# A decoder block on one core: VectorE's weight low parts booked beside GpSimd in the planner, and the last query tile's scores as three products of 352 columns

## The chip, the cores and the metric

One core of one Trainium2 chip. The metric is the device time of one execution in microseconds; the time before is 654.11 us, the median of three runs (653.83 to 655.35).

## What is computed

One transformer block on 512 tokens of width 1024, all in float32: a norm, projections, two kinds of attention, output projection with norm and residual, a gated feed-forward part with a short convolution (width 2816), and an embedding gate (PLE). What matters here is the attention with compressed, selected and window branches ("nsa", 8 heads in 2 groups), and the sliding-window attention ("swa", 8 heads in 2 groups):

```python
s_c = einsum(q, k_cmp) * scale - slope * dist_c      # 31 compressed keys
p_c = softmax(s_c) * valid_c                         # o_c = p_c @ v_cmp
s_s = einsum(q, k_selected) * scale - slope * dist   # causal; 512 tokens have 8 blocks, all are selected
s_w = einsum(q, k_window) * scale - slope * dist     # causal, window 512
o = g0 * o_c + g1 * o_s + g2 * o_w
...
mix = concat(o_nsa, o_swa) @ w_o
x = x + rmsnorm(mix); h = rmsnorm(x); gu = h @ w_gate_up
```

## The kernel before

**Arithmetic.** A float32 operand is split into a high part, rounded to the matmul's own format, and a low part, the rest; a product is three matmuls, high x high, low x high, high x low. ScalarE makes a weight's high part (`hi`, `oh`), VectorE or GpSimd subtracts it from the raw weight to give the low part (`lo` at L1056 for 1024 columns; `low` at L967 for 512 columns of the output projection, on GpSimd for its first half and on VectorE for its second).

**Units.** Attention runs as 16 units, `ORDER`: the nsa kind before the swa kind, group 0 before group 1, and query tiles of 128 tokens in the order 3, 0, 2, 1. A unit has four heads r. For each head TensorE makes scores (`s`, L584 and L585: the query against the keys' high and low parts), VectorE adds the distance bias and takes the minimum in one pass (`m`, `soft`, L588: a custom operation and a read of its accumulator), ScalarE exponentiates in place (`e`, L592), VectorE takes reciprocals (`rc`, L689, L755), and GpSimd scales the rows (`g`, `scale_rows`, L580). Then, block by block of 128 keys, TensorE transposes four heads' probabilities (`t`, L782), ScalarE makes the high part (`h`, L786), VectorE the low part (`l`, L790), and TensorE multiplies by the values (`v`, L797). The unit's sum is added up, split (`up`, `ad`, `oh`, `ol`; L840, L847, L852, L856) and kept for the output projection. GpSimd also normalizes the compressed branch (`px`, `gc`, `pm`).

In an nsa unit the key tiles `kn` lie as 32 compressed keys, then 512 keys of one branch, then 512 of the other, 1056 columns in a row. For query tile 3 (units 0 and 4) the scores of one head are three products into three PSUM banks: 256 columns, of which the first 32 are used, and twice 512. VectorE takes three passes: over 32, 512 and 512 columns.

**Fill work.** Beside the units TensorE has matmuls of large rank that it runs when nothing of the units is ready: projections of queries and keys (`f`, L247 to L251; ended by `fe`, then moved to other partitions by 4 or 8 transfers `fm` on SP, L924), the output projection's first half, which needs the nsa mixes alone, and its second half with the swa mixes (`op`, L976 to L978; phases "fill" and "outproj"), and the eight PLE products of six matmuls (`pl`, L1087 to L1090). Loads go over SP's queue (`w` L883, `ow` L959, `ld` L1049, `x1` L1073). After the units come the squares and their sum (`sq`, `sa`), the norm's column and row (`col` L1110, `row` L1123), per chunk `n1`, `n2`, `nh` (L1140), `nl`, `nq`, and the first gate and up products (`ma`, L1163).

**The planner.** From the start of the units to those products, the order of the work is made by a list scheduler in the kernel's own code (`Plan`, with `add` and `order`). Each operation has an engine, an estimated length, a rank, what it comes after, and the buffers that it takes and uses. A step picks, on each engine, the operation of lowest rank that can start when the engine is free (otherwise the one that can start first), and emits over all engines the one that starts first. The estimates decide the order alone: every engine runs its queue in that order, and waits on the chip only for data and buffers. The ranks of the units count in units: about i - 1 + r/4 for scores and softmax of unit i, i and more for its products; fill has 1000 and more. `SHIFT` adds to a rank below 100, by the first letters and the length of an operation's name: ("hi", 2) is the high part of the norm's weights, ("e", 4) an nsa exponential, ("e", 3) an swa one, ("pe2", 2) the eviction of a PLE product. The high parts of the norm's weights have ranks 15.0, 15.2 and 15.4 for p and the two PLE weights and 16.5 to 17.1 for the first gate and up weights before the shift; `lo` is 0.1 behind.

Of the kernel before, what the change touches and what calls it, by code (L numbers as in the profile page):

```python
# [15 lines left out]
P = 128  # L16
# [46 lines left out]
PAIRS = 2  # L63
UNITS = 3
SHIFT = {("px", 2): 0.26, ("sa", 2): -0.78, ("l", 4): 0.71, ("pe2", 2): -1.35, ("v", 4): 1.33, ("e", 4): 1.34,
         ("ol", 3): -0.84, ("oe", 3): 0.38, ("ol", 2): 1.32, ("e", 3): 0.21, ("sq", 2): -0.62, ("s", 4): 0.18,
         ("pm", 2): 1.23, ("t", 3): 0.43, ("lo", 2): -0.03, ("oh", 3): -0.25, ("hi", 2): 0.71}
# [7 lines left out]
class Plan:  # L75

# [14 lines left out]
    def add(self, name, eng, us, rank, f, after=(), take=(), use=(), land=0.0):  # L91
# [3 lines left out]
        self.ops[name] = (eng, us, rank, f, [a for a in after if a], list(take), land)  # L95
# [5 lines left out]
    def order(self, free):  # L101
# [28 lines left out]
        while len(out) < len(ops):  # L130
            best = None
            for eng, names in todo.items():
                pick, f = None, free.get(eng, 0.0)
                for name in names:
# [3 lines left out]
                    t = max(r, f)  # L138
# [10 lines left out]
            free[eng] = t + op[1]  # L149
            done[name] = t + op[1] + op[6]  # L150
# [21 lines left out]
class Block:  # L172
# [136 lines left out]
    def move(self, dst, src):  # L309
        self.nc.sync.dma_start(dst.bitcast(F32), src.bitcast(F32))  # L310
# [283 lines left out]
    def plan_units(self, plan, qready):  # L594
# [10 lines left out]
        for i, (kind, g, qt) in enumerate(units):  # L605
# [32 lines left out]
            if kind == "n":  # L638
# [5 lines left out]
                segs = {0: [(0, 160, 2)], 3: [(0, 256, 1), (NCMP, T, 1), (NCMP + T, T, 1)]}.get(  # L644
                    qt, [(0, NCMP + n, 1), (NCMP + T, n, 1)])
                for r in range(4):
# [18 lines left out]
                    for b, seg in enumerate(segs):  # L665
# [7 lines left out]
                    where = {0: [(0, 0, NCMP), (0, NCMP, n), (0, 160, n)], 3: [(0, 0, NCMP), (1, 0, n), (2, 0, n)]}.get(  # L673
                        qt, [(0, 0, NCMP), (0, NCMP, n), (1, 0, n)])
                    for b, (sb, c0, w) in enumerate(where):

                        def soft(r=r, b=b, sb=sb, c0=c0, w=w, u=u, per=per, n=n, slope=slopes[r], bias=(cb if b == 0 else bias)):
                            dst = u["pc"][:, r, :] if b == 0 else u["pk", r // per][:, r % per, b - 1, :n]
                            self.soft(dst, u["ps", r, sb][:, c0 : c0 + w], bias, slope, 3e38, u["nm"][:, r, b : b + 1])

                        op(("m", i, r, b), "DVE", soft_us(w), x + 0.01 * (b == 2), soft, [("s", i, r, sb)], (), [("ps", i, r, sb)])
# [190 lines left out]
    def plan_projections(self, plan, order, due, given):  # L872
# [4 lines left out]
        for n, f in enumerate(order):  # L877
# [65 lines left out]
            for m in range(moves):  # L943
                a(("fm", f, m), "SP", 0.5, rank - 50, lambda m=m, move=move: move(m), [("fe", f, 2)],
                  [("u", ("q", f))] if m == 0 and f != 8 else [], [("ft", f)], land=1.8)
# [776 lines left out]
```

## Time and profile before

| | us |
|---|---|
| median of three runs | 654.11 |
| the profiled execution | 655.55 |
| its span, from the first to the last instruction | 653.8 |
| TensorE busy | 641.0 (98%) |
| VectorE busy | 483.6 (74%) |
| ScalarE busy | 365.2 (56%) |
| GpSimd busy | 148.7 (23%) |
| mean granted clock of TensorE | 0.995 of full speed |

PE is TensorE, DVE VectorE, ACT ScalarE, POOL GpSimd, SP the engine that only issues transfers. The units run from about 74 to 220 us; the first gate and up products begin at 249.6 us. A matmul's length in the rows is longer than its pitch, since matmuls overlap: pitches are read from start to start. Each row of a timeline is: start in us, length in us (of all instructions that it merges, xN), engine, line, operation, tiles written and read, shapes, and in brackets the idle time before it and what ended it.

### The profile page before, as it was taken

The page shows a single profiled execution, that of the slowest core. Times are in us where ns is not written, and L with a number is a line of the kernel's source. Part 1 is how long each engine was busy: PE and PEld are TensorE (multiplying, and loading weights), DVE is VectorE, ACT ScalarE, POOL GpSimd, SP SyncE. Part 2 cuts the span into 40 slices and gives each one's busy share as a digit, 9 for nine tenths or more (in the row PEclk, how much of TensorE's full clock was granted, in tenths as well). Part 3 has the DMA queues.
Part 4 walks back from the last instruction along what each step waited for, and adds up shares of the span by engine and source line. Part 5 has one row for each costly group of instructions (what it writes and reads, how often), then busy time and mean ns, then how long its engine had stood idle before and what let it go on. Part 6 is the DMA issues. An engine that isn't in the chain of part 4 may idle for free.

```text
span 653.8 us, 10319 instructions
## 1 busy us (share of the span) xinstructions
PE 641.0 (98%) x3709; PEld 562.3 (86%) x3709; DVE 483.6 (74%) x994; ACT 365.2 (56%) x709; POOL 148.7 (23%) x223
## 2 busy tenths in 40 slices
PE   8999999999998999999998999999999999999996
PEld 7988888888886888888888999999998888889985
DVE  6794769988896469689899999999857333233972
ACT  6554779889998366265555556556636322222341
POOL 1112597668476230021320000000000000010000
PEclk9999999999999999999999999999999999999999
DMA  8437623110236159203323334233263454331031
GB/s 300 149 118 222 180 81 85 45 50 26 72 106 234 48 178 321 97 34 96 130 97 119 91 115 129 71 125 129 57 201 113 145 217 126 110 96 65 1 131 63
DMA packets 27282, 78.01 MB, mean 119 GB/s; under 512 B 3424, under 2 KB 4704, under 8 KB 27232
## 3 DMA queue, kind: packets, MB, share of 16 engines
q1 hardware_dynamic: 27088, 77.28, 36.5%
q8 instruction: 29, 0.48, 0.3%
q14 instruction: 21, 0.17, 0.1%
q10 hardware_dynamic: 144, 0.08, 0.1%
HBM read 63.72 MB, written 6.29 MB: 107 GB/s over the span
## 4 chain that ended last, share of the span: by engine, by line
PE 81%; DVE 9%; ACT 5%; issue 2%; POOL 2%; DMA 1%; ACTq 0%; DVEq 0%
PE mlpdown_pss L247 3%; PE mlpdown_pss L251 3%; PE mlpdown_pss L250 3%; PE strassen_pss L1415 3%; PE strassen_pss L1418 3%; PE strassen_pss L1419 3%; PE nsa_pst L782 2%; PE nsa_pso L797 2%; PE mlpdown_psmm L247 2%; PE mlpdown_psmm L250 2%; PE mlpdown_psmm L251 2%; PE r_pss L1163 2%; PE r_psmm L1163 2%; PE strassen_pst L1418 2%; PE strassen_pst L1415 2%
## 5 line engine op out<-in xcount | busy, mean ns | idle before, releaser
L232 DVE TENSOR_TENSOR mlpdown_wh<-mlpdown_wr,mlpdown_wh 128x1024 fp32r<-128x1024 f32 (+1 forms) x28 | 32.5, 1166 | 48.2 <-ACT mlpdown_wh L228 47.2
L228 ACT ACTIVATE mlpdown_wh<-mlpdown_wr 128x1024 fp32r<-128x1024 f32 (+1 forms) x28 | 27.8, 998 | 63.6 <-PE mlpdown_pss L250 23.0
L303 POOL TENSOR_TENSOR mlpdown_s<-mlpdown_s,mlpdown_s 128x512 f32<-128x512 f32 x6 | 7.8, 1293 | 238.2 <-ACT mlpdown_s L302 238.2
L580 POOL TENSOR_SCALAR nsa_u<-nsa_u,nsa_nrc,gate 128x512 f32<-128x512 f32 (+3 forms) x64 | 38.3, 612 | 22.1 <-DVE nsa_nrc L689 16.0
L1415 PE MATMUL strassen_pss<-sums_u,strassen_u 128*128 128x256 f32 x144 | 40.5, 282 | 1.7 <-ACT strassen_s L1426 1.7
L1418 PE MATMUL strassen_pss<-sums_u,strassen_u 128*128 128x256 f32 x144 | 40.5, 281 | 0.0
L1419 PE MATMUL strassen_pss<-sums_u,strassen_u 128*128 128x256 f32 x144 | 40.5, 281 | 0.0
L592 ACT ACTIVATE nsa_u<-nsa_u,nsa_nnm 128x512 f32<-128x512 f32 (+3 forms) x64 | 35.2, 552 | 1.9 <-DVE nsa_nnm L588 1.8
L790 DVE TENSOR_TENSOR nsa_u<-nsa_pst,nsa_u 128x512 fp32r<-128x512 f32 x40 | 27.0, 688 | 10.0 <-ACT nsa_u L786 9.6
L1377 DVE TENSOR_TENSOR strassen_u<-strassen_u,strassen_u 128x1024 fp32r<-128x1024 f32 x27 | 33.3, 1236 | 0.0
L247 PE MATMUL mlpdown_pss<-mlpup_u,mlpdown_wh 128*128 128x512 f32 (+1 forms) x88 | 32.0, 364 | 0.0
L251 PE MATMUL mlpdown_pss<-mlpup_u,mlpdown_wh 128*128 128x512 f32 (+1 forms) x88 | 32.0, 363 | 0.0
L250 PE MATMUL mlpdown_pss<-mlpup_u,mlpdown_wh 128*128 128x512 f32 (+1 forms) x88 | 32.0, 363 | 0.0
L588 DVE CUSTOM_DVE_ANT_0 nsa_u<-nsa_pss,biastables_u 128x512 f32<-128x512 f32 (+3 forms) x64 | 29.6, 483 | 1.3 <-PE nsa_pss L585 1.1
L1373 ACT ACTIVATE strassen_u<-strassen_u 128x1024 fp32r<-128x1024 f32 x27 | 28.4, 1051 | 1.6 <-DVE strassen_u L1389 1.4
L1415 PEld LDWEIGHTS strassen_pss<-sums_u,strassen_u 128*128 128x128 f32 x144 | 27.2, 189 | 1.9 <-ACT strassen_s L1426 1.9
L797 PE MATMUL nsa_pso<-nsa_u,vnatural_u 128*128 128x512 f32 x80 | 27.3, 420 | 0.1
L1418 PEld LDWEIGHTS strassen_pss<-sums_u,strassen_u 128*128 128x128 f32 x144 | 27.2, 189 | 0.1
L1419 PEld LDWEIGHTS strassen_pss<-sums_u,strassen_u 128*128 128x128 f32 x144 | 27.2, 189 | 0.0
L786 ACT ACTIVATE nsa_u<-nsa_pst 128x512 fp32r<-128x512 f32 x40 | 23.2, 594 | 6.1 <-PE nsa_pst L782 5.8
L1309 POOL TENSOR_TENSOR mlpup_s<-mlpup_s,r3b 128x512 f32<-128x512 f32 x7 | 14.0, 2000 | 47.8 <-ACT mlpup_s L1281 42.8
L1418 PE MATMUL strassen_pst<-sums_u,strassen_u 128*128 128x256 f32 x88 | 24.8, 281 | 0.0
(545 smaller groups left out, 2306.4 us busy)
## 6 DMA issues: line engine op xcount, KB each, us to landing
mlpdown_wr<-in_down_dram SPq DMA_DIRECT2D x16, 512.0 KB, 3.7
strassen_wr<-in_gu_dram SPq DMA_DIRECT2D x14, 512.0 KB, 4.6
strassen_u<-in_gu_dram SPq DMA_DIRECT2D x14, 512.0 KB, 4.0
mlpup_wr<-in_gu_dram SPq DMA_DIRECT2D x10, 512.0 KB, 3.4
mlpdown_wr<-in_down_dram SPq DMA_DIRECT2D x8, 384.0 KB, 3.2
projq_wr<-in_win_dram SPq DMA_DIRECT2D x5, 512.0 KB, 3.3
loadx_u<-in_xT_dram SPq DMA_DIRECT2D x8, 256.0 KB, 5.0
compress_u<-projk_u SPq DMA_DIRECT2D x16, 128.0 KB, 2.3
```

What stands on the lines that cost most here:

```text
L232: l = eng.tensor_sub(lw, raw, hi.bitcast(F32))
L247: r = mm(ps, hi, x[:, 0, :], start=start, stop=False)
L250: mm(ps, lo, x[:, 0, :], start=False, stop=False)
L251: mm(ps, hi, x[:, 1, :], start=False, stop=stop)
L580: self.tc.keep_in_program_order(self.nc.gpsimd.tensor_scalar(ap, ap, col, gate, op0=ALU.mult, op1=ALU.mult))
L588: self.tc.keep_in_program_order(self.nc.vector.tensor_tensor_reduce(dst, src, bias, op0=ALU.add, op1=ALU.min, scale=slope, scalar=first, a ...
L592: self.tc.keep_in_program_order(self.nc.scalar.activation(p, p, AF.Exp, bias=nm, scale=-1.0, accum_out=sm))
L797: keep(nc.tensor.matmul(u["po"], v, u["t", j][:, part, :], start=start, stop=u["left"] == 0))
L1377: keep(sub(lo, src, hi.bitcast(F32)))
L1415: r = mm(ps, hi[:, o], x[:, 0, :], start=fresh and p == 0, stop=False, skip_group_check=not fresh)
L1418: mm(ps, lo[:, o], x[:, 0, :], start=False, stop=False, skip_group_check=not fresh)
L1419: mm(ps, hi[:, o], x[:, 1, :], start=False, stop=p == Q - 1, skip_group_check=not fresh)
```

## The change

- `Plan.add` has a new field, `beside`: another engine that an operation keeps from working. `Plan.order` starts such an operation no earlier than that engine is free, and books the engine until the operation's end. It is set to GpSimd for VectorE's low parts of the second half of the output projection (`ol`) and for the low parts of the norm's weights (`lo`). No instruction and no wait on the chip comes from it.
- For query tile 3 of the nsa units, the scores of a head are three products of 352 columns (`THIRD`). The two passes over 512 columns now lie across two banks each: 320 and 192 columns, 160 and 352. The first piece is a new operation `n`, whose minimum goes into a small tile that the second piece, `m`, takes as its initial value.
- The transfers `fm` of a projection are planned one after the other's landing. The loads `ld` and `x1` are planned at 1.6 us of SP, not 0.8.
- `SHIFT` is another table.

```diff
+THIRD = (NCMP + 2 * T) // 3
 UNITS = 3
-SHIFT = {("px", 2): 0.26, ("sa", 2): -0.78, ("l", 4): 0.71, ("pe2", 2): -1.35, ("v", 4): 1.33, ("e", 4): 1.34,
-         ("ol", 3): -0.84, ("oe", 3): 0.38, ("ol", 2): 1.32, ("e", 3): 0.21, ("sq", 2): -0.62, ("s", 4): 0.18,
-         ("pm", 2): 1.23, ("t", 3): 0.43, ("lo", 2): -0.03, ("oh", 3): -0.25, ("hi", 2): 0.71}
+SHIFT = {("l", 4): 0.88, ("pe2", 2): -4.0, ("v", 4): 1.95, ("oe", 3): -1.52, ("e", 3): 1.52, ("s", 4): -0.33,
+         ("pm", 2): 1.91, ("pn", 2): -0.47, ("g", 4): 1.14, ("oh", 2): 0.97, ("fe", 3): 0.12, ("rc", 3): -1.18,
+         ("gc", 2): 1.04, ("m", 4): 0.11, ("n", 4): -2.1}
...
-    def add(self, name, eng, us, rank, f, after=(), take=(), use=(), land=0.0):
+    def add(self, name, eng, us, rank, f, after=(), take=(), use=(), land=0.0, beside=None):
         assert name not in self.ops, name
         if rank < 100:
             rank += SHIFT.get((name[0], len(name)), 0.0)
-        self.ops[name] = (eng, us, rank, f, [a for a in after if a], list(take), land)
+        self.ops[name] = (eng, us, rank, f, [a for a in after if a], list(take), land, beside)
...
-                    t = max(r, f)
+                    t = max(r, f, free.get(ops[name][7], 0.0))
...
             free[eng] = t + op[1]
+            if op[7]:
+                free[op[7]] = t + op[1]
...
-                segs = {0: [(0, 160, 2)], 3: [(0, 256, 1), (NCMP, T, 1), (NCMP + T, T, 1)]}.get(
+                segs = {0: [(0, 160, 2)], 3: [(k * THIRD, THIRD, 1) for k in range(3)]}.get(
...
+                    where = {0: [[(0, 0, NCMP)], [(0, NCMP, n)], [(0, 160, n)]],
+                             3: [[(0, 0, NCMP)], [(0, NCMP, THIRD - NCMP), (1, 0, T + NCMP - THIRD)],
+                                 [(1, T + NCMP - THIRD, 2 * THIRD - T - NCMP), (2, 0, THIRD)]]}.get(
+                        qt, [[(0, 0, NCMP)], [(0, NCMP, n)], [(1, 0, n)]])
+                    for b, pieces in enumerate(where):
+                        d0 = 0
+                        for e, (sb, c0, w) in enumerate(pieces):
+                            last = e == len(pieces) - 1
+
+                            def soft(r=r, b=b, sb=sb, c0=c0, w=w, u=u, per=per, e=e, d0=d0, last=last, slope=slopes[r],
+                                     bias=(cb if b == 0 else bias)):
+                                dst = u["pc"][:, r, :] if b == 0 else u["pk", r // per][:, r % per, b - 1, d0 : d0 + w]
+                                if not last:
+                                    u["nt", b] = self.tiny([P, 1], f"nt{b}")
+                                self.soft(dst, u["ps", r, sb][:, c0 : c0 + w], bias[:, d0 : d0 + w], slope, u["nt", b] if e else 3e38,
+                                          u["nm"][:, r, b : b + 1] if last else u["nt", b])
+
+                            op(("m" if last else "n", i, r, b), "DVE", soft_us(w), x + 0.01 * (b == 2), soft,
+                               [("s", i, r, sb), ("n", i, r, b) if e else None], (), [("ps", i, r, sb)])
+                            d0 += w
...
+                  lambda c=c, half=half: low(c, half, nc.vector if half else nc.gpsimd), [("oh", c, half)], (), [("oraw", c, half)], beside="POOL" if half else None)
...
-                a(("fm", f, m), "SP", 0.5, rank - 50, lambda m=m, move=move: move(m), [("fe", f, 2)],
+                a(("fm", f, m), "SP", 0.5, rank - 50, lambda m=m, move=move: move(m), [("fe", f, 2), ("fm", f, m - 1) if m else None],
...
-            op(("ld", key), "SP", 0.8, 2880 + n if early else 3000 + n, lambda key=key, src=src, room=room: load(key, src, room),
+            op(("ld", key), "SP", 1.6, 2880 + n if early else 3000 + n, lambda key=key, src=src, room=room: load(key, src, room),
...
-            op(("lo", key), "DVE", 1.135, rank + 0.1, lambda key=key: low(key, nc.vector), [("hi", key)], (), [("raw", key)])
+            op(("lo", key), "DVE", 1.135, rank + 0.1, lambda key=key: low(key, nc.vector), [("hi", key)], (), [("raw", key)], beside="POOL")
...
-            op(("x1", j), "SP", 0.8, 3100 + j, lambda j=j: back(j), [end, ("x1", j - 1) if j else None], [("p", ("x1", j))], land=2.2)
+            op(("x1", j), "SP", 1.6, 3100 + j, lambda j=j: back(j), [end, ("x1", j - 1) if j else None], [("p", ("x1", j))], land=2.2)
```

## Rows read from the trace of the kernel before

**Rows 1.** The page, busy times of the whole span: busy us (share of the span) and instructions of each engine.

```profile
PE 641.0 (98%) x3709; PEld 562.3 (86%) x3709; DVE 483.6 (74%) x994; ACT 365.2 (56%) x709; POOL 148.7 (23%) x223
```

**Rows 2.** Busy time by stretches (start:end in us): length, then busy us and instructions of TensorE, its weight loads, VectorE, ScalarE and GpSimd; the granted clock of TensorE, the DMA engines' share, GB/s.

```profile
100.00:200.00 100.00, 98.71 (x568) 81.86 (x567) 87.51 (x332) 90.62 (x267) 69.46 (x124) 1.00 0.26 73
...
206.40:210.00 3.60, 1.44 (x9) 0.79 (x8) 3.29 (x4) 2.12 (x5) 3.60 (x4) 1.00 0.29 96
210.00:213.80 3.80, 3.80 (x13) 2.98 (x12) 3.25 (x5) 1.90 (x3) 0.14 (x1) 0.55 0.29 92
213.80:250.00 36.20, 36.20 (x166) 29.73 (x165) 20.54 (x28) 19.00 (x31) 9.41 (x10) 1.00 0.44 146
```

**Rows 3.** Waits of TensorE over the whole span: who waited for whom, us in total, times, longest.

```profile
PE swa_pst L782 <- POOL swa_u L580: 2.2, 2, 1.6
PE strassen_pss L1415 <- ACT strassen_s L1426: 1.7, 1, 1.7
...
PE swa_pst L782 <- DVE compressout_u L809: 0.4, 1, 0.4
```

**Rows 4.** Timeline of TensorE, 195 to 220 us.

```profile
200.56 1.04 PE L782 MATMUL swa_pst<-ident,swa_u 128*128 128x128 f32 x8
201.35 0.48 PE L976 MATMUL fill_psmm<-nsa_u,swa_u 128*128 128x512 f32 x1
...
206.43 0.57 PE L782 MATMUL swa_pst<-ident,swa_u 128*128 128x128 f32 x2
208.61 0.33 PE L782 MATMUL swa_pst<-ident,swa_u 128*128 128x128 f32 x1 [1.61 <-POOL swa_u L580]
209.50 0.77 PE L782 MATMUL swa_pst<-ident,swa_u 128*128 128x128 f32 x5 [0.56 <-POOL swa_u L580]
210.02 0.49 PE L976 MATMUL fill_psmm<-nsa_u,swa_u 128*128 128x512 f32 x1
...
213.72 0.41 PE L976 MATMUL fill_psmm<-nsa_u,swa_u 128*128 128x512 f32 x1
```

**Rows 5.** Timeline of GpSimd, 184 to 217 us.

```profile
198.23 1.84 POOL L580 TENSOR_SCALAR swa_u<-swa_u,swa_rc 128x256 f32<-128x256 f32 x4 [1.66 <-DVE swa_rc L755]
...
204.67 4.78 POOL L580 TENSOR_SCALAR swa_u<-swa_u,swa_rc 128x256 f32<-128x256 f32 x4 [1.31 <-DVE swa_rc L755]
```

**Rows 6.** Timeline of VectorE, 195 to 252 us.

```profile
205.05 2.65 DVE L1056 TENSOR_TENSOR r_u<-r_u,r_u 128x1024 fp32r<-128x1024 f32 x2 [0.48 <-ACT r_u L1053]
207.62 1.48 DVE L967 TENSOR_TENSOR swa_u<-swa_wr,swa_u 128x512 fp32r<-128x512 f32 x2
...
242.47 1.23 DVE L1056 TENSOR_TENSOR r_u<-r_wr,r_u 128x1024 fp32r<-128x1024 f32 x1 [0.26 <-ACT r_u L1053]
```

**Rows 7.** Timeline of TensorE, 75 to 126 us: score products of an nsa unit, 320, 256 and 512 columns.

```profile
80.80 0.30 PE L584 MATMUL nsa_pss<-compress_u,projq_u 128*128 128x320 f32 x1
...
81.09 0.30 PE L584 MATMUL nsa_pss<-compress_u,projq_u 128*128 128x320 f32 x1
...
116.25 0.28 PE L584 MATMUL nsa_pss<-compress_u,projq_u 128*128 128x256 f32 x1
...
116.48 0.39 PE L584 MATMUL nsa_pss<-compress_u,projq_u 128*128 128x512 f32 x1
116.71 0.39 PE L585 MATMUL nsa_pss<-compress_u,projq_u 128*128 128x512 f32 x1
```

**Rows 8.** Timeline of VectorE, 75 to 182 us: passes of 32 and 128 columns with a constant initial value, an operation that reads what the one before it wrote (L697, L699), and a pass of 128 columns with an initial value from a tile. READ_ACCUMULATOR starts where the pass's own pitch ends.

```profile
79.86 0.18 DVE L588 CUSTOM_DVE_ANT_0 nsa_pc<-nsa_pss,biastables_u 128x32 f32<-128x32 f32 x1
...
79.97 0.28 DVE L588 CUSTOM_DVE_ANT_0 nsa_u<-nsa_pss,biastables_u 128x128 f32<-128x128 f32 x1
80.18 0.08 DVE L588 DVE_READ_ACCUMULATOR2_ANT nsa_nnm<- 128x1 f32 x1
...
84.57 0.29 DVE L697 TENSOR_REDUCE nsa_nsm<-nsa_pc 128x4 f32<-128x128 f32 x1 [0.19 <-issue]
84.96 0.23 DVE L699 RECIPROCAL nsa_nrc<-nsa_nsm 128x12 f32<-128x12 f32 x1
...
166.18 0.35 DVE L588 CUSTOM_DVE_ANT_0 swa_u<-swa_pss,biastables_u,nsink 128x128 f32<-128x128 f32 x1
166.45 0.08 DVE L588 DVE_READ_ACCUMULATOR2_ANT swa_nm<- 128x1 f32 x1
```

**Rows 9.** Timeline of ScalarE, 195 to 252 us.

```profile
203.47 0.51 ACT L592 ACTIVATE swa_u<-swa_u,swa_nm 128x257 f32<-128x257 f32 x1
...
203.96 1.05 ACT L1053 ACTIVATE r_u<-r_u 128x1024 fp32r<-128x1024 f32 x1
...
248.87 0.72 ACT L1140 ACTIVATE r_u<-r_u,cols 128x512 fp32r<-128x512 f32 x1
```

**Rows 10.** Timeline of TensorE, 218 to 252 us: the first matmul of the first PLE product, that of the next one, and the last matmul of the last one.

```profile
220.81 0.40 PE L1087 MATMUL r_pss<-r_u,r_u 128*128 128x512 f32 x1
...
238.52 0.40 PE L1087 MATMUL r_psmm<-r_u,r_u 128*128 128x512 f32 x1
...
249.34 0.39 PE L1090 MATMUL r_pss<-r_u,r_u 128*128 128x512 f32 x1
```

**Rows 11.** Timeline of SP's queue, 60 to 250 us: the four transfers of the query projection that the plan makes first.

```profile
84.92 5.52 SPq L924 DMA_DIRECT2D nsa_u<-fill_u  x4
```


## What the change does to the time, predicted blind

> **What bounds the kernel now.** I read five views, in this order. The busy times say that TensorE is busy for 641.0 us, 98% of the span [rows 1]: a change gains only by taking work from TensorE or by closing one of its few gaps. The table by stretches says where the gaps lie [rows 2]: 1.3 us are spread over 100 to 200 us, 2.2 us of the 3.6 us from 206.4 us on are idle, in the next 3.8 us the granted clock is 0.55, and from 213.8 to 250 us nothing is lost. TensorE's waits name the releaser [rows 3]: the largest, 2.2 us in two pieces, is the transposes of the last sliding-window unit waiting for GpSimd's row scaling (L580). Then the timelines. TensorE's eight transposes of that unit take from 206.43 to 210.02 us, 3.59 us, where eight at 200.56 us take 0.79 us: 2.80 us lost. The nine matmuls behind them, at half clock (1.2 of 2.4 GHz) after that idle time, take 3.70 us, against 9 x 0.23 = 2.07 at the pitch of the 512-column products [rows 4, 7]: 1.63 us lost. The place costs 4.4 us. GpSimd shows why: four row scalings, 1.84 us at 198.23 us, take 4.78 us at 204.67 us [rows 5], just while VectorE runs two 1024-column subtractions of SBUF tiles (2.65 us for the pair, alone 1.23 each) and two of 512 columns [rows 6]. Each engine slows the other, GpSimd most. The planner knew nothing of it; it is the thing that the first half of the change teaches it.
>
> **The change part by part.**
>
> *Three products of 352 columns.* Per head TensorE now streams 256 + 512 + 512 columns twice. Pairs of starts give 0.115 us for 256, 0.23 for 512 and 0.145 for 320 columns [rows 7], so 0.00045 per column and 0.159 for 352. Per head: 2 x (0.115 + 0.23 + 0.23) = 1.15 before, 2 x 3 x 0.159 = 0.95 after; eight heads (four in each of the two units with query tile 3) save 8 x 0.196 = **1.6 us** of TensorE. It is on the path, because TensorE hardly waits there.
>
> *Five minimum passes instead of three.* VectorE gets 16 instructions more. A pass of 32 columns, nearly all fixed cost, has a pitch of 0.11 us; an initial value from a tile instead of a constant adds 0.27 - 0.21 = 0.06; an operation that reads what the one just before it wrote starts 0.10 us after its end instead of 0.07 before it [rows 8], so 0.17 more if both pieces stand together. 16 x 0.17 = 2.7 us to 16 x 0.34 = 5.4 us of VectorE, half of it in each unit. VectorE is busy 87.5 of the 100 us around the second unit and ScalarE 90.6 [rows 2], so most is hidden; the cover is the queue of projection matmuls, which need no softmax. On TensorE I put 0.5 us, nearest to what these passes cost it now (part of 1.3 us in the row); the ends are 0 and 2.7 (one unit's whole share at its dearest). A gain is excluded: nothing is taken from VectorE. A score bank is now read by up to two or three passes before it comes free; the work per head in the three banks is the same, so this is inside that bound. Queued behind a second piece that waits for its product are the low parts (L790), for which transposed products wait.
>
> *Low parts planned beside GpSimd.* No instruction is added or removed. The new field is not a wait: it moves the start that the planner books for these VectorE operations to GpSimd's free time and books GpSimd for their length; what reaches the chip is the order in each queue. If the order keeps the subtractions off the last units' scalings, or has TensorE do its twelve ready output-projection matmuls first, **4.4 us** come back. The ends are 0 and 4.4.
>
> *The new ranks.* The largest shift at the tail, worked out by hand: the first three high parts of the norm's weights (`hi`) had ranks 15.71 to 16.11 and the last unit's exponentials (`e`, length 3) 14.21 to 14.96; now they are 15.0 to 15.4 and 15.52 to 16.27. ScalarE ran the exponentials before the high parts (203.47, then 203.96 us) [rows 9]; now it prefers the high parts. Their low parts then fall into the time of the exponentials, ahead of the reciprocal and of the scalings: this is what should part the two engines. Its price is up to 3 x 1.05 = 3.2 us of lateness for the last unit, to be covered by matmuls that are ready: the twelve behind the transposes (2.7 us) and the first halves of the late output projection. I expect the end of that cover to show as two unit-boundary waits like today's 0.4 us [rows 3], **1.0 us** with what surrounds them; ends 0 and 3.2.
>
> *Moves and loads.* The four or eight transfers of a projection are booked one after the other's landing, and the late loads at 1.6 instead of 0.8 us of SP. On SP's queue each group is already issued in a row (four in 5.52 us, some of it waiting) [rows 11], and no wait of TensorE names a transfer. The planned arrival moves later by 3 x 1.8 = 5.4 us for four moves, which shifts scores behind fill matmuls, not the chip's arrival; the hazard is a move now queued on SP behind a weight load that waits for its buffer. I take 0, ends -0.3 (a wait of the middle stretch fewer) and +0.6.
>
> *After the plan.* From 250 us on TensorE has one wait, 1.7 us for ScalarE [rows 3]; the code there is the same, so time saved ahead passes through. I take 0.
>
> **Sum.** -1.6 - 4.4 + 0.5 + 1.0 + 0 = -4.5 us. The profiled execution took 655.55 us (span 653.84 and 1.7 around it), 1.44 above the median of the runs; the change gives 651.1 by that and **649.6** by the median, 654.11 - 4.5.
>
> By the Trainium skill, page "SBUF — State Buffer", its section on the single rule of the shared port pair, VectorE and GpSimd share one pair of ports as an exclusive lock, a VectorE operation with two SBUF inputs contends with a GpSimd operation that reads SBUF, and issue order decides who blocks. The trace agrees on the collision: 4.78 instead of 1.84 us. The rule speaks against the change: an order without a wait leaves the subtractions free to start whenever their inputs are there, and by it the first rival below would follow.
>
> **The rivals.** *The order is no wait.* With nothing else queued between the reciprocal and the subtractions, VectorE starts them at once although the planner booked them after GpSimd, and the collision is as before. For it: that is how the four stood in VectorE's queue at 205 us, and the low parts that the transposes release come later in any plan. Against it: the ranks above put the high parts, which release them, ahead of the exponentials, and a planner that knows the price places the transposes behind the ready matmuls. It keeps the 4.4 us: 654.11 - 1.6 + 0.5 = **653.0**.
>
> *The last unit comes too late (slower).* TensorE's cover at the end is used up to the microsecond. One PLE product already stands at 220.81 us, before the last output projection can go on; the other seven, from 238.52 to 249.6 us with the norm's small matmuls among them [rows 10], hide the norm's chain, whose first scaled tile is ready at 248.87 + 0.72 = 249.59 us [rows 9]. A PLE product (six matmuls, 1.36 us) pulled forward to fill a hole opens it again there. If the high parts make the exponentials 3.2 us late and the old hole stays, whether there or moved to the norm, the result is -1.6 + 0.5 + 3.2 = +2.1, and with a second stretch at half clock (1.6) +3.7: **656.2 to 657.8**, centre 657.0. It decides once the lateness that isn't covered passes the 1.1 us that the columns leave net while the hole stays, or 5.5 us if the hole goes.
>
> *More comes back.* The plan also closes the 1.3 us of the middle stretch [rows 2] and costs neither 0.5 nor 1.0: 654.11 - 1.6 - 4.4 - 1.3 = **646.8**.
>
> **How the numbers follow.** Forecast 0.56, order-no-wait 0.22, slower 0.14, more 0.08. The range: the forecast's own bounds are 648.1 (no new cost) and about 652.2 (2.7 for the passes and 1.4 at the tail); with the first rival at 653.0 and its passes up to 2.7 us it must reach 654.5, and downwards past 646.8: 646.5 to 654.5, leaving out the slower case and little else. A difference of 0.3% (2.0 us) is about what a measurement of this kernel can tell from no change. Faster by more is the forecast, the better case and a small part of the first rival: 0.66; within it most of the first rival: 0.21; slower by more: 0.13.
>
> **What would show it.** Right: the scores of query tile 3 as 352 columns at a pitch near 0.16 us; the last units' scalings at 0.46 us each; no TensorE wait over 1 us between 200 and 215 us and a clock of 1.00 there; a norm that still starts without a gap. The first rival: L580 groups of four at over 3 us beside L1056. The second: idle TensorE before the transposes of the last unit, or between the PLE products and L1163. Wrong in its sizes, if TensorE waits for L588 in the two units with tile 3, or if the wait after 250 us changes from 1.7 us though no code there did.

## The result and the profile after

The median is 651.42 us (650.65 to 653.12, 11 runs) against 655.62 us of the kernel before, run beside it (653.64 to 657.95, 11 runs): a ratio of 0.9935 with a 95% interval of 0.992 to 0.9949. That is 4.2 us faster; 4.5 us were forecast. In this comparison the kernel before ran 1.5 us longer than the 654.11 us from which the forecast of 649.6 starts, so the difference and the ratio are what to compare. The executions of one kernel fall into groups some 2 us apart (with the booking alone 653.1 to 653.3 and 654.9 to 655.4 us), so a median can land on either group, and the ratio, taken over all runs, is the steadier number. The profiled execution took 651.38 us (span 649.7), against 655.55 (653.8).

The page of the kernel after, its busy times (answers to [rows 1]):

```profile
PE 638.0 (98%) x3709; PEld 560.6 (86%) x3709; DVE 484.7 (75%) x1026; ACT 366.2 (56%) x709; POOL 146.1 (22%) x223
```

Busy time by stretches, the kernel after (columns as in [rows 2]):

```profile
100.00:200.00 100.00, 98.19 (x571) 81.81 (x570) 87.41 (x345) 90.92 (x268) 69.64 (x126) 1.00 0.25 72
200.00:220.00 20.00, 19.86 (x91) 15.99 (x90) 15.17 (x23) 14.58 (x26) 8.03 (x10) 1.00 0.47 156
220.00:250.00 30.00, 30.00 (x138) 24.53 (x137) 18.73 (x27) 16.98 (x28) 7.13 (x8) 1.00 0.62 214
```

Waits of TensorE over the whole span, the kernel after (columns as in [rows 3]):

```profile
PE strassen_pss L1430 <- ACT strassen_s L1441: 1.6, 1, 1.6
...
PE nsa_pss L588 <- DVE nsa_nnm L592: 0.5, 2, 0.3
PE swa_pst L797 <- DVE compressout_u L824: 0.4, 1, 0.4
```

The wait for GpSimd's scaling is gone, and so are the idle stretch and the half clock at 206 to 214 us: from 200 to 220 us TensorE is busy 19.86 of 20 us at a granted clock of 1.00. Not everything is gain: 100 to 200 us holds 98.19 busy us where it held 98.71 [rows 2], and VectorE's passes appear among the waits (0.5 us for `nsa_nnm`, 0.3 before). The one wait at a boundary of sliding-window units is 0.4 us, as before; the second one that the prediction expected at the tail didn't come.

Where the 4.1 us of span went, by the starts of TensorE's matmuls (for each of them the distance to the next start, less the usual distance for its shape, added up; I call this the excess): between 200 and 220 us the excess falls from 4.45 to 0.64, **-3.8**; over the rest of 60 to 275 us it rises by **+1.2**; the narrower score products give **-1.5**. The sum is -4.1, the difference of the spans.

Timeline of TensorE, the kernel after: products of one head of query tile 3, then the last sliding-window unit's transposes.

```profile
74.30 0.32 PE L588 MATMUL nsa_pss<-compress_u,projq_u 128*128 128x352 f32 x1
74.45 0.32 PE L589 MATMUL nsa_pss<-compress_u,projq_u 128*128 128x352 f32 x1
74.61 0.32 PE L588 MATMUL nsa_pss<-compress_u,projq_u 128*128 128x352 f32 x1
...
203.05 0.60 PE L797 MATMUL swa_pst<-ident,swa_u 128*128 128x128 f32 x4
...
203.97 0.66 PE L797 MATMUL swa_pst<-ident,swa_u 128*128 128x128 f32 x4
```

Timeline of GpSimd, the kernel after: the last unit's four scalings.

```profile
199.41 0.48 POOL L584 TENSOR_SCALAR swa_u<-swa_u,swa_rc 128x256 f32<-128x256 f32 x1 [1.19 <-DVE swa_rc L770]
...
200.56 0.49 POOL L584 TENSOR_SCALAR swa_u<-swa_u,swa_rc 128x256 f32<-128x256 f32 x1
...
202.28 0.94 POOL L584 TENSOR_SCALAR swa_u<-swa_u,swa_rc 128x256 f32<-128x256 f32 x2
```

Timeline of VectorE, the kernel after: the passes of one head, the last unit's reciprocal, an addition with one SBUF and one PSUM input, and the first subtraction of the norm's weights.

```profile
73.12 0.48 DVE L592 CUSTOM_DVE_ANT_0 nsa_u<-nsa_pss,biastables_u 128x320 f32<-128x320 f32 x1
73.53 0.08 DVE L592 DVE_READ_ACCUMULATOR2_ANT nsa_nt<- 128x1 f32 x1
73.53 0.32 DVE L592 CUSTOM_DVE_ANT_0 nsa_u<-nsa_pss,biastables_u 128x160 f32<-128x160 f32 x1
...
73.89 0.41 DVE L592 CUSTOM_DVE_ANT_0 nsa_u<-nsa_pss,biastables_u,nsa_nt 128x192 f32<-128x192 f32 x1
...
74.22 0.58 DVE L592 CUSTOM_DVE_ANT_0 nsa_u<-nsa_pss,biastables_u,nsa_nt 128x352 f32<-128x352 f32 x1
74.73 0.09 DVE L592 DVE_READ_ACCUMULATOR2_ANT nsa_nnm<- 128x1 f32 x1
...
199.13 0.18 DVE L770 RECIPROCAL swa_rc<-swa_sm 128x4 f32<-128x4 f32 x1 [0.57 <-ACT swa_u L596]
...
202.63 0.69 DVE L1002 TENSOR_TENSOR swa_u<-swa_u,fill_psmm 128x512 f32<-128x512 f32 x1
...
205.19 1.22 DVE L1071 TENSOR_TENSOR r_u<-r_u,r_u 128x1024 fp32r<-128x1024 f32 x1
```

Timeline of ScalarE, the kernel after: the last unit's fourth exponential and the first high part.

```profile
198.51 0.49 ACT L596 ACTIVATE swa_u<-swa_u,swa_nm 128x257 f32<-128x257 f32 x1
...
203.01 1.05 ACT L1068 ACTIVATE r_u<-r_u 128x1024 fp32r<-128x1024 f32 x1
```

All four scalings are over at 203.2 us, 2 us before the first large subtraction starts: each takes its usual 0.47 to 0.49 us, and TensorE's waits no longer name them. The parting came about in another way than I had worked out. The exponentials still run *before* the high parts; the last unit's softmax came forward (scalings at 199.41 instead of 204.67 [rows 5]) while the first high part hardly moved (203.01 instead of 203.96 [rows 9]). It is the softmax alone: the unit's first score product starts at 191.92 us, before at 192.04, but from there to the last reciprocal it is 7.2 us instead of 12.4. The time is gained on ScalarE, whose last exponential starts 2.1 us after the last minimum pass (196.37 to 198.51) instead of 8.1 (195.36 to 203.47). Nor was a high part ready to go ahead of the exponentials: the load of p, which the first one reads, lands at 200.1 us.

In the passes, the first pieces of both halves come first. Between each read-out of `nsa_nt` and the piece that takes it as initial value stand two other passes, and no gap opens.

### The profile page after: what moved, and what is told of

The parts are those of the page before. It is cut to its first block, busy times and chain, and to the rows that moved or that the text cites. A ratio compares the mean times of both kernels' runs of the same rounds, so it can differ in the third digit from the quotient of the medians.

```text
span 649.7 us, 10374 instructions
## 1 busy us (share of the span) xinstructions
PE 638.0 (98%) x3709; PEld 560.6 (86%) x3709; DVE 484.7 (75%) x1026; ACT 366.2 (56%) x709; POOL 146.1 (22%) x223
## 4 chain that ended last, share of the span: by engine, by line
PE 72%; DVE 15%; ACT 5%; issue 3%; DMA 2%; POOL 1%; SPq 1%; ACTq 0%; DVEq 0%
PE mlpdown_pss L251 3%; PE mlpdown_pss L255 3%; PE mlpdown_pss L254 3%; PE strassen_pss L1430 3%; PE strassen_pss L1433 3%; PE strassen_pss L1434 3%; PE mlpdown_psmm L251 2%; PE mlpdown_psmm L255 2%; PE mlpdown_psmm L254 2%; PE nsa_pst L797 2%; PE nsa_pso L812 2%; PE r_pss L1178 2%; PE r_psmm L1178 2%; PE strassen_pst L1430 2%; PE strassen_pst L1433 2%
## 5 line engine op out<-in xcount | busy, mean ns | idle before, releaser
L592 DVE CUSTOM_DVE_ANT_0 nsa_u<-nsa_pss,biastables_u 128x320 f32<-128x320 f32 (+3 forms) x64 | 24.7, 413 | 0.6 <-PE nsa_pss L589 0.6
L797 PEld LDWEIGHTS nsa_pst<-ident,nsa_u 128*128 128x128 f32 x160 | 18.9, 140 | 6.8 <-DVE nsa_u L805 1.2
```

Of the source, the lines that this page charges most:

```text
L797: keep(nc.tensor.transpose(pt[:, r * P : (r + 1) * P], src, self.ident))
```

## The experiments

My theory: the collision of VectorE and GpSimd is what cost 4.4 us, and its removal, with the columns, is the gain. Open were which edit removes it, what the pieces cost, and whether the rest is worth anything.

**1. The booking alone** (the kernel before with the planner's new field and nothing else):

```diff
-                    t = max(r, f)
+                    t = max(r, f, free.get(ops[name][7], 0.0))
...
+            if op[7]:
+                free[op[7]] = t + op[1]
```

> The kernel before with the booking of GpSimd alone (the field beside and its two uses); ranks, scores and SP as before. Theory that the booking is no wait and that it was the new ranks that parted the engines: no gain, ratio 1.000 or above; the subtractions still stand right behind the last reciprocal in VectorE's queue, now four in a row, and the last unit's scalings take 4.8 us or more again. Rival, the booking parts them by itself: the wait of TensorE for L580 goes, 3.5 to 4.4 us faster, ratio about 0.994.

Measured: 0.9976 (0.9962 to 0.9991), 654.96 us against 655.27 (the profiled execution, 653.08, is 1.9 below the median). That lies between my theory (1.000 or above) and its rival (0.994). Its timelines of GpSimd, VectorE and TensorE in turn:

```profile
204.47 4.77 POOL L582 TENSOR_SCALAR swa_u<-swa_u,swa_rc 128x256 f32<-128x256 f32 x4 [1.31 <-DVE swa_rc L757]
```

```profile
204.85 2.64 DVE L1058 TENSOR_TENSOR r_u<-r_u,r_u 128x1024 fp32r<-128x1024 f32 x2 [0.48 <-ACT r_u L1055]
```

```profile
207.13 0.50 PE L978 MATMUL fill_psmm<-nsa_u,swa_u 128*128 128x512 f32 x1 [0.73 <-ACT r_u L987]
...
210.66 1.04 PE L784 MATMUL swa_pst<-ident,swa_u 128*128 128x128 f32 x8
...
247.47 0.73 PE L1165 MATMUL r_pss<-r_u,r_u 128*128 128x512 f32 x2 [1.29 <-ACT r_u L1142]
```

The collision is untouched, 4.77 us as before: the order is no wait, as the first rival said. But TensorE's eight transposes now stand behind ready projection matmuls, at 210.66 instead of 206.43 us [rows 4], and TensorE no longer waits for the scalings. Two new waits give back 2.0 us of that. The second is the rival of the tail: PLE products were taken early, at 217 to 219.5 us, none is left to cover the norm's chain, and TensorE waits 1.29 us there.

**2. Without the booking** (the kernel after, `beside` left out of both calls):

```diff
-                  ..., [("oh", c, half)], (), [("oraw", c, half)], beside="POOL" if half else None)
+                  ..., [("oh", c, half)], (), [("oraw", c, half)])
...
-               ..., lambda key=key: low(key, nc.vector), [("hi", key)], (), [("raw", key)], beside="POOL")
+               ..., lambda key=key: low(key, nc.vector), [("hi", key)], (), [("raw", key)])
```

> The changed kernel without the booking (ranks, scores and SP as changed). Theory: the same as the changed kernel within 1 us, 3 to 4 us faster than before, no wait of TensorE over 1 us between 195 and 215 us. Rival, the booking parts the engines: the collision is back, scalings at over 4 us, and only the columns' 1.1 to 1.6 us are left.

Measured: 0.9929 (0.9913 to 0.9945), 651.4 us, span 649.7 us, the same as the kernel after. With the new ranks the booking changes nothing that can be measured in the time.

**3. The new ranks alone** (the kernel before with the new table):

```diff
-SHIFT = {("px", 2): 0.26, ("sa", 2): -0.78, ("l", 4): 0.71, ...
+SHIFT = {("l", 4): 0.88, ("pe2", 2): -4.0, ("v", 4): 1.95, ...
```

> The kernel before with the new table of ranks alone; no booking, scores and SP as before. Theory: the ranks alone put the low parts of the transposes of the last but one unit between the last reciprocal and the subtractions, so the collision and the 2.2 us wait go: 3 to 4 us faster, ratio about 0.995. Rival, the booking is needed: the wait for L580 stays above 1.5 us and the ratio is 0.999 to 1.001.

Measured: 0.9989 (0.9969 to 1.0009), no difference that is clear of noise, where my theory said 0.995. Its timeline of GpSimd, then TensorE's waits:

```profile
203.04 1.84 POOL L580 TENSOR_SCALAR swa_u<-swa_u,swa_rc 128x256 f32<-128x256 f32 x4 [1.07 <-DVE swa_rc L755]
```

```profile
PE swa_pso L797 <- ACT swa_u L786: 0.9, 1, 0.9
...
PE swa_pst L782 <- DVE compressout_u L809: 0.7, 1, 0.7
```

Here the collision *is* gone (1.84 us for four, VectorE's first large subtraction follows at 206.69 us), so it is the ranks that part the engines. They shorten the last unit's softmax here too: from its first score product to the last reciprocal 7.3 us, against 12.4 before. In this run the first high part also starts later, 0.42 us after ScalarE ran dry, when the load of p has landed (205.59 us). But other waits, 0.9 and 0.7 us (0.4 before) among them, take most of the gain back: the excess falls by 2.9 us between 200 and 220 us and grows by about 1.8 us elsewhere.

**4. The old ranks in the kernel after** (the reverse edit):

```diff
-SHIFT = {("l", 4): 0.88, ("pe2", 2): -4.0, ("v", 4): 1.95, ...
+SHIFT = {("px", 2): 0.26, ("sa", 2): -0.78, ("l", 4): 0.71, ...
```

> The changed kernel with the old table of ranks (booking, scores, passes and SP as changed). Theory: the ranks carry the change, by the place of the first pieces above all; without them the second pieces follow their first ones again (3.7 us of VectorE), the collision stays and the booking only moves TensorE's transposes behind ready matmuls: ratio 0.999 to 1.004. Rival, booking and scores bring the gain and the ranks are only a retouch: ratio 0.995 or less.

Measured: 1.0075 (1.0051 to 1.0098), 660.43 us against 655.23: dearer than any theory had it. Its timeline of TensorE, and two stretches behind (columns as in [rows 2]):

```profile
253.41 0.73 PE L1178 MATMUL r_pss<-r_u,r_u 128*128 128x512 f32 x2 [3.12 <-ACT r_u L1155]
```

```profile
253.40:254.90 1.50, 1.49 (x6) 1.26 (x7) 1.50 (x3) 1.36 (x3) 0.00 (x0) 0.92 0.94 281
254.90:258.30 3.40, 3.40 (x9) 2.62 (x9) 3.33 (x6) 1.79 (x4) 0.00 (x0) 0.53 0.94 290
```

The second rival in full: the PLE products are used up, TensorE stands still for 3.1 us before the first gate and up products, and soon after runs at half clock, eight distances from start to start in 3.40 us instead of 8 x 0.23 = 1.84. What the passes of the next experiment cost comes on top. And with the old ranks the collision is back, booking or not: the last unit's four scalings take 3.84 us, and its softmax 11.6 us from the first score product to the last reciprocal.

**5. The 352-column scores alone** (the kernel before with `THIRD` and the pieces; old ranks, so that `n` has the rank of `m`):

```diff
-                segs = {0: [(0, 160, 2)], 3: [(0, 256, 1), (NCMP, T, 1), (NCMP + T, T, 1)]}.get(
+                segs = {0: [(0, 160, 2)], 3: [(k * THIRD, THIRD, 1) for k in range(3)]}.get(
```

> The kernel before with the three products of 352 columns and the split passes alone; ranks, booking and SP as before. Theory: the columns pass to the end nearly whole, 1.6 us less TensorE and 0 to 0.5 us given back, so 1.1 to 1.6 us faster, ratio about 0.998; the wait of TensorE for L580 near 206 us stays at 2.2 us and the four scalings at over 4 us, because nothing at the tail is changed. Rival: the 2.2 us that VectorE has more eat the columns: ratio 1.000.

Measured: 1.005 (1.0033 to 1.0068), 659.44 us against 655.27: slower, although TensorE streams less; my theory said 0.998, its rival 1.000. One head in VectorE's timeline of the kernel before, then of this one:

```profile
72.93 0.18 DVE L588 CUSTOM_DVE_ANT_0 nsa_pc<-nsa_pss,biastables_u 128x32 f32<-128x32 f32 x1
...
74.26 0.08 DVE L588 DVE_READ_ACCUMULATOR2_ANT nsa_nnm<- 128x1 f32 x1
```

```profile
72.76 0.18 DVE L589 CUSTOM_DVE_ANT_0 nsa_pc<-nsa_pss,biastables_u 128x32 f32<-128x32 f32 x1
...
73.28 0.08 DVE L589 DVE_READ_ACCUMULATOR2_ANT nsa_nt<- 128x1 f32 x1
73.51 0.42 DVE L589 CUSTOM_DVE_ANT_0 nsa_u<-nsa_pss,biastables_u,nsa_nt 128x192 f32<-128x192 f32 x1
...
74.09 0.08 DVE L589 DVE_READ_ACCUMULATOR2_ANT nsa_nt<- 128x1 f32 x1
74.32 0.58 DVE L589 CUSTOM_DVE_ANT_0 nsa_u<-nsa_pss,biastables_u,nsa_nt 128x352 f32<-128x352 f32 x1
74.83 0.09 DVE L589 DVE_READ_ACCUMULATOR2_ANT nsa_nnm<- 128x1 f32 x1
```

First and second piece stand back to back, and the second starts 0.23 us after the read-out's start (73.28 to 73.51) where independent operations start with it. A head takes 72.76 to 74.83, 2.07 us, against 1.33 before (72.93 to 74.26) and 1.61 after (73.12 to 74.73). Over eight heads that is 5.9 us more of VectorE than before, against 2.2 in the kernel after. TensorE's excess between 60 and 200 us grows by 4.9 us; between 200 and 220 us, where nothing was changed, it stays (four scalings in 4.78 us).

**6. The scores alone, first pieces ahead** (the kernel of 5 with one entry more):

```diff
-SHIFT = {("px", 2): 0.26, ...
+SHIFT = {("n", 4): -2.1, ("px", 2): 0.26, ...
```

> The kernel before with the three products and the split passes, as in the run with the scores alone (ratio 1.005), and only the rank of the first pieces from the new table (-2.1), so that VectorE runs the two first pieces, the 32 columns and then the two second pieces. Theory: the 0.23 us that each second piece waits for the minimum just in front of it, 16 x 0.23 = 3.7 us of VectorE, are gone; the columns then pass: ratio 0.996 to 0.999, unless the new order at the tail collides elsewhere. Rival, the split itself costs what the columns give: ratio 1.003 or more.

Measured: 0.9989 (0.9973 to 1.0004), 654.48 us: 4 to 5 us below the kernel of 5 (by the ratios and by the medians) through that one rank. The tail also changed (its four scalings took 3.87 us, not 4.78), so not all of it is the passes'.

**7. The pieces together in the kernel after** (the first piece issued right in front of the second, all else equal):

```diff
-                                self.soft(dst, ...)
+                                if not last:
+                                    u["first", r, b] = piece
+                                    return
+                                if e:
+                                    u["first", r, b]()
+                                piece()
```

> The changed kernel with each first piece issued right in front of its second piece; ranks, booking and plan as changed. Theory: VectorE has 16 x 0.23 = 3.7 us more, and TensorE waits more in the two units with query tile 3: 1 to 4 us slower than the changed kernel, ratio to before 0.995 to 1.000. Rival, it was the order of other work that made the scores alone slow: within 0.5 us of the changed kernel, ratio 0.9935.

Measured: 0.9974 (0.9957 to 0.999), 653.74 us, 2.3 us over the 651.4 of the kernel after. Its waits of TensorE:

```profile
PE nsa_pss L588 <- DVE nsa_nnm L592: 0.7, 2, 0.4
...
PE nsa_pss L588 <- DVE nsa_nt L592: 0.5, 2, 0.3
```

So the place of the first pieces is worth 2 to 3 us in the kernel after, more than the columns' 1.5.

**8. Two subtractions of SBUF tiles behind the last reciprocal** (the kernel after; 896 columns each, on a table that isn't used any more):

```diff
+                    if i == len(ORDER) - 1:
+                        for k in range(2):
+                            keep(nc.vector.tensor_sub(self.dist_all, self.dist_all, self.dist_all))
```

> The changed kernel with two more subtractions of two SBUF inputs (896 columns, some 1.1 us each) in VectorE's queue right behind the last reciprocal, on a table that is no longer used; the plan is unchanged. VectorE is idle for 1.76 us there, so its own work is late by 0.4 us at most. Theory, the shared ports: the last unit's scalings, 0.48 us each, take 1 us or more while the two run, TensorE waits over 0.5 us for L584 or L797's inputs, and 0.5 to 3 us are lost against the changed kernel. Rival, that VectorE's time alone counts: within 0.4 us of the changed kernel and the same as the next run.

Measured: 0.9955 (0.9939 to 0.997), 652.08 us.

**9. Two reductions in the same place**, about as long but with one input:

```diff
+                            keep(nc.vector.tensor_reduce(self.dist_all[:, k : k + 1], self.dist_all[:, 2:], axis=..., op=ALU.add))
```

> The control: the changed kernel with two more reductions of one SBUF input (894 columns, about 1.0 us each) at the same place of VectorE's queue. Theory, the shared ports: the scalings stay at 0.46 to 0.5 us and the time is that of the changed kernel within 0.5 us. Rival, that VectorE's time alone counts: as slow as the run with two subtractions.

Measured: 0.9938 (0.9914 to 0.9962), 650.87 us. GpSimd and VectorE of 8, then of 9:

```profile
200.91 1.23 POOL L585 TENSOR_SCALAR swa_u<-swa_u,swa_rc 128x256 f32<-128x256 f32 x1 [1.18 <-DVE swa_rc L772]
202.10 1.57 POOL L878 TENSOR_TENSOR swa_u<-swa_s,swa_u 128x256 fp32r<-128x256 f32 x1
```

```profile
200.73 2.35 DVE L775 TENSOR_TENSOR biastables_u<-biastables_u 128x896 f32<-128x896 f32 x2
```

```profile
199.10 0.48 POOL L585 TENSOR_SCALAR swa_u<-swa_u,swa_rc 128x256 f32<-128x256 f32 x1 [1.18 <-DVE swa_rc L772]
199.56 0.74 POOL L878 TENSOR_TENSOR swa_u<-swa_s,swa_u 128x256 fp32r<-128x256 f32 x1
```

```profile
198.93 2.05 DVE L775 TENSOR_REDUCE biastables_u<-biastables_u 128x1 f32<-128x894 f32 x2
```

This is the collision, made at a chosen place. Beside two-input subtractions a scaling takes 1.23 us instead of 0.48 and a GpSimd subtraction 1.57 instead of 0.74; beside reductions neither changes. So it isn't VectorE's being busy. The reductions differ in a second way, since they write one column where the subtractions write 896; the kernel after settles that: beside L1002, which writes 512 columns of SBUF and reads one input from SBUF and one from PSUM (202.63 us), two scalings take their usual 0.94 us (202.28 us). It is the second SBUF input that does it. The delay showed as two waits of TensorE of 0.5 us each (one names L585, one VectorE's L869); the reductions gave none. The times, 652.08 and 650.87 us, differ in that direction, but their intervals overlap: shown is the longer scaling, not a loss of time.

**10. The old booking of SP** (the kernel after, moves and loads as before):

```diff
-                a(("fm", f, m), "SP", 0.5, ..., [("fe", f, 2), ("fm", f, m - 1) if m else None],
+                a(("fm", f, m), "SP", 0.5, ..., [("fe", f, 2)],
...
-            op(("ld", key), "SP", 1.6, ...
+            op(("ld", key), "SP", 0.8, ...
...
-            op(("x1", j), "SP", 1.6, ...
+            op(("x1", j), "SP", 0.8, ...
```

> The changed kernel with SP planned as before (transfers not in a chain, loads at 0.8 us). Theory: SP's estimates move nothing that TensorE waits for: the changed kernel's time within 0.7 us, ratio 0.9935. Rival: they are what makes the loads at the tail arrive in time, and 1 us or more is lost.

Measured: 0.9966 (0.9952 to 0.998), 652.46 us: 1 us over the kernel after by the medians and 2 by the ratios, and the interval lies just above that kernel's (0.992 to 0.9949). My theory, no loss, fails; the rival has the size right. Its new wait of TensorE, at 212.59 us:

```profile
PE swa_pso L812 <- ACT swa_u L801: 1.1, 1, 1.1
```

No wait over 0.3 us names a transfer, so the rival's reason, late loads, isn't what the waits show. A product waits for a high part in ScalarE's queue; that the estimates of SP put it late there by the order they give is my reading, not shown by a run of its own.

**11 and 12. A planner that knows the chain** (the kernel after; 0.23 us between `n` and `m` and 0.06 us more for a piece with an initial value, and `SHIFT` fitted anew to that; 11 and 12 have two tables that this planner rates equal):

```diff
-                since[n] = max(since[n], done[name] + (0.0 if e == eng else ...
+                since[n] = max(since[n], done[name] + ((0.23 if name[0] == "n" else 0.0) if e == eng else ...
...
-                            op(("m" if last else "n", i, r, b), "DVE", soft_us(w), ...
+                            op(("m" if last else "n", i, r, b), "DVE", soft_us(w) + (0.06 if e else 0.0), ...
```

> A version that the runs point to: the changed kernel, the planner also told of the 0.23 us that a second piece waits for a first one just in front of it and of the 0.06 us of an initial value from a tile, and ranks that fit this. Theory: the columns are in full, the second pieces stand apart, the last scalings and the subtractions too, and no PLE product is taken early: as fast as the changed kernel or up to 2 us faster, ratio 0.990 to 0.9935. Rival: what is left between planned and real order is not in these costs, and another order opens other waits: ratio 0.994 to 0.998.

> As the run before, with a second, unlike set of ranks that the same planner rates as equal. Theory: within 1 us of it, ratio 0.990 to 0.9935. Rival: the two differ by more than 1 us, since the order is then decided by what the planner does not know.

Measured: 0.9918 (0.9898 to 0.9938), 650.0 us, and 0.995 (0.9932 to 0.9967), 651.89 us. The first is as forecast and has the lowest median of all kernels here, but its interval overlaps that of the kernel after. The second misses the forecast. It waits, in TensorE's waits,

```profile
PE nsa_pst L788 <- POOL nsa_pc L730: 0.8, 1, 0.8
```

at a place where the first doesn't. By the medians, what the planner rates equal comes out 1.9 us apart; the two intervals just overlap.

## Why the prediction was right, and which of its steps were not

The time fell 4.2 us where 4.5 were forecast, and the forecast's case is the one that happened: the collision went, the columns came in, something was given back. That the sum fits to 0.3 us is partly luck: the tail came out 0.4 us better than forecast and the passes and what else lies outside the tail 0.7 us worse. Term by term:

| term | forecast | measured |
|---|---|---|
| columns of the scores | -1.6 | -1.5 |
| the stretch with the collision, less its cover | -4.4 + 1.0 | -3.8 |
| passes, in the units | +0.5 | +1.2 with all else outside the tail |
| SP | 0 | the old booking is 1 to 2 us worse; its wait lies in the stretch of the second row |
| sum | -4.5 | -4.1 (spans), -4.2 (medians) |

**Columns: right.** 352 columns have a pitch of 0.15 to 0.16 us (74.30, 74.45, 74.61), as interpolated. Experiment 5 shows that this gain is not safe by itself.

**The collision: right in its place and price, wrong in what removes it.** The step that failed is the one on the new ranks: "now it prefers the high parts. Their low parts then fall into the time of the exponentials". ScalarE did the opposite. I compared the ranks of four operations, as if all were ready together; in the kernel after the data of the first high part landed only when the exponentials were over. What counted was how fast the last unit's softmax got through ScalarE's queue: the new table shortens it by 5 us, from 12.4 to 7.3 us alone and to 7.2 in the kernel after. Which of the fifteen entries does it was not tried. The step on the booking said that the 4.4 us come back if the subtractions keep off the scalings *or* if TensorE takes its ready matmuls first. Both ways exist: the first in experiment 3 and in the kernel after, the second in experiment 1. What I put first in the change, the booking, isn't needed for the result.

By the Trainium skill, page "SBUF — State Buffer", section on who interferes with whom, a VectorE operation with two SBUF inputs contends with a GpSimd operation that reads SBUF, while one with at most one SBUF input, outside the two-port modes, does not. Experiments 8 and 9 agree: 1.23 against 0.48 us.

**The first rival** had its premise right (an order does not hold the subtractions back: 4.77 us in experiment 1) and its conclusion wrong, since the transposes had moved.

**The second rival** was real, and its price about right: 3.2 us of hole and 1.6 of half clock were forecast, 3.1 and 1.6 came in experiment 4. That this run is dearer than the rival's 656.2 to 657.8 us isn't the hole's doing: between 60 and 200 us the excess is also 5 us larger than before, as in experiment 5. In experiment 1 the hole came to 1.29 us. The new ranks avoid it (TensorE is busy 30.00 of 30 us from 220 to 250 us).

**Passes: a size that was too low at one end.** I allowed 0.17 us for a piece that directly follows the one it depends on; it is 0.23 (0.15 us after the read-out's end instead of 0.08 before it). The kernel after escapes it by the rank of `n`, an entry of the table that I had read as tuning and not as part of this edit. At the rank of `m`, 5.9 us of VectorE come with 4.9 us more excess of TensorE in the units, beyond my bound of 2.7; the span of experiment 5 is 3.9 us longer, although the narrower products save 1.5.

**SP: a term put at nothing that isn't.** I took 0, with 0.6 us as the worst, because no wait of TensorE named a transfer. Taking the new estimates out costs 1 to 2 us (experiment 10), and without them the excess between 200 and 220 us is 1.4 us larger. So part of the 3.8 us at the tail hangs on them; that it goes through the order of another engine's queue is argued, not shown.

**What stays open.** The edits don't add. Alone three of them give +0.5% (scores), -0.24% (booking) and -0.11% (ranks, within noise), +0.15% in all; together with the fourth, the estimates of SP, which wasn't tried alone, -0.65%. Each edit reshuffles the whole order, and waits of 0.5 to 1 us come and go with it. The +1.2 us outside the tail I can locate (the units from 70 to 130 us) but not give to one cause: experiment 11, whose planner knows more of the passes' cost, has 1.7 us less of this excess over all of 60 to 275 us (7.3 against 9.0), yet its table differs everywhere.

## What to carry to other kernels

When two engines slow each other, look first for ready work of the engine that waits for them: in experiment 1 moving the waiting instruction behind it brought most of what parting the two brought there, 3.3 of 3.8 us between 200 and 220 us; but ready work that is used up is missing later, 1.29 us at the norm. A split that makes one operation depend on the one just before it needs a place for the first half well ahead of the second; ask for it in the order, not only in the code. And test the parts of a change to a planner in the presence of the others, since edits that gain together can gain nothing or lose alone.

## What the hardware showed that I had not expected

- A read-out of VectorE's accumulator, used as the next operation's initial value, holds that operation 0.23 us from the read-out's start; with two other passes between, nothing.
- Granted clock: before 250.3 us of experiment 4 TensorE ran without a gap at 1.00; after 3.1 us of standing still it had 0.92 for 1.5 us, then 0.53 for 3.4 us (starts 0.43 us apart, the level of 1.2 GHz), then 1.00 again. After the 1.3 us of standing still in experiment 1 it kept 1.00.
- Of two engines that collide, the one that comes second waits, and its row includes the wait. The second scaling of the kernel before starts beside a subtraction that ends at 206.27 us, and itself ends 0.35 us after that; the third and the fourth fare alike, 0.26 and 0.35 us after the subtraction in front, so all four take 4.78 us. In the kernel after it once goes the other way: GpSimd's subtraction L871 ends at 210.88 us, and VectorE's, which starts beside it, takes 1.76 us instead of 1.22. So the price isn't a ratio; it is about what the other engine's operation still has to run. GpSimd paid more at the tail because its short operations stood behind long ones. First the pair of the kernel before (timelines of VectorE from 205.1 to 206.2 us and of GpSimd from 205.2 to 206.5, each cut to the one instruction), then that of the kernel after:

```profile
205.05 1.23 DVE L1056 TENSOR_TENSOR r_u<-r_u,r_u 128x1024 fp32r<-128x1024 f32 x1 [0.48 <-ACT r_u L1053]
205.12 1.50 POOL L580 TENSOR_SCALAR swa_u<-swa_u,swa_rc 128x256 f32<-128x256 f32 x1
```

```profile
209.88 1.00 POOL L871 TENSOR_TENSOR swa_u<-swa_s,swa_u 128x256 fp32r<-128x256 f32 x1 [4.72 <-ACT swa_u L867]
210.20 1.76 DVE L1071 TENSOR_TENSOR r_u<-r_u,r_u 128x1024 fp32r<-128x1024 f32 x1
```
